# Turning the gated product with DVE blocks and DMAs through DRAM instead of TensorE transposes, in four feed-forwards

## The chip, the cores and the metric

The kernel runs on one core of one Trainium2 chip. The metric is the device time of one execution in microseconds (us), the median over several runs. PE is TensorE (its weight loads are shown apart as PEld), DVE is VectorE, ACT is ScalarE, POOL is GpSimd, and SP issues most of the DMAs.

## The reference

A two-layer trunk over 256 tokens of width 1024. Each layer is half a feed-forward, a token mixer, half a feed-forward; layer 0 mixes with a convolution module, layer 1 with latent attention. So there are four feed-forwards, all of this kind:

```
def swiglu_ffn(h, w1, w3, w2):
    return (jax.nn.silu(h @ w1) * (h @ w3)) @ w2
...
h = h + 0.5 * swiglu_ffn(rmsnorm(h, ffn_norm1[i]), ffn1_w1[i], ffn1_w3[i], ffn1_w2[i])
```

`w1` and `w3` are 1024 x 2816, `w2` is 2816 x 1024, everything in float32. The product `silu(..) * (..)`, 256 x 2816, is called the gated product here. The second multiplication contracts over its 2816 columns, so TensorE needs it with the columns on the partitions: it has to be turned.

## The kernel before

Float32 precision is reached with three matmuls for each product (`mm3`, L226 to L232): each operand is kept as a rounded part (`hi`, `Xh`, `Gh`) and a remainder (`lo`, `Xl`, `Gl`).

Weights come in blocks of 1 MB. SP loads each into a `raw` tile (three buffers), ACT rounds it into `hi` (L164), DVE makes `lo` (L165); `hi` and `lo` have four buffers each. SP issues its DMAs in the order in which they stand, and each waits there for its buffer, so a DMA at the head of SP's queue holds all behind it.

A feed-forward (`ffn_in`, L487) has two stages. The first goes over six chunks `c` of the 2816 columns: chunks 0 to 4 have 512 columns of `w1` and of `w3`, four weight blocks each; chunk 5 has 256 of each in two blocks. One block feeds 24 matmuls: 4 row tiles of the weights, two halves of 128 tokens (`tb`), three matmuls each. The four sums `u[m, tb]` of a chunk lie in the four PSUM banks of tag "A". After the chunk, ACT makes `s = silu(u[0, tb])` (L533) and DVE makes `g = s * u[1, tb]` (L535), 128 tokens x 512 columns, and a chunk's bank is free for a later one once its `s` and `g` are made. In chunk 5 both factors lie in one bank, so it uses two banks.

In `flush` PE transposes `g` in squares of 128 (L262, by `transposed`) into a PSUM bank of tag "B", four for a `g` of 512 columns and two for one of 256; ACT rounds the result into `Gh` (L497) and DVE writes `Gl` (L498). That is done early in the next chunk, for chunk 5 in the first block of the second stage.

The second stage (`Rows`) goes over 11 blocks of `w2`; block `i` contracts over column tiles 2i and 2i+1 of `Gh` and `Gl`. Its four sums `o` use the four "A" banks, the first two from chunk 4's later pair and the last two from chunk 5's. Blocks 9 and 10 are done in `finish`. Chunk 4's columns are needed from block 8 on, chunk 5's in block 10.

The order on each engine is set by a scheduler when the program is built, from the order of the code, from priorities (`urgent`) and from its own estimate of durations. Each engine then runs its instructions in that order.

Of the kernel before, what the change touches and what calls it, by code (L numbers as in the profile page):

```python
# [11 lines left out]
F32 = mybir.dt.float32  # L12
# [7 lines left out]
P = 128  # L20
# [59 lines left out]
def trunk(ctx: ExitStack, tc: tile.TileContext, x, pos, invf, gains, gfin, wdw,  # L80
          f1w13, f1w2, f2w13, f2w2, cw1, cw2, wa, wuq, wukv, wo, out):
    nc = tc.nc
# [4 lines left out]
    xp = ctx.enter_context(tc.tile_pool(name="x", bufs=1))  # L87
    tmp = ctx.enter_context(tc.tile_pool(name="tmp", bufs=2))
    small = ctx.enter_context(tc.tile_pool(name="small", bufs=4))
    ps = ctx.enter_context(tc.tile_pool(name="ps", bufs=1, space=bass.MemoryType.PSUM))  # L90

    n_uid = [0]

    def uid(s):
        n_uid[0] += 1
        return f"{s}_{n_uid[0]}"
# [4 lines left out]
    def bank(tag, name):  # L101
        return ps.tile([P, 512], F32, tag=tag, name=uid(name), bufs=BANKS[tag])
# [5 lines left out]
    for i in range(2):  # L108
        for w13, w2 in ((f1w13, f1w2), (f2w13, f2w2)):
# [6 lines left out]
            if w13 is f1w13:  # L116
                if i == 0:


                    for m in (-1, -2, 0, 1, 2, 3, 4, 5, 6, 7, -3, -4):  # L120
                        w = cw2[-m - 1] if m < 0 else cw1[m]
# [11 lines left out]
    def order(ins, first):  # L133
        tc.add_manual_dep(ins.ins, first.name, mybir.DependencyInfo(
            mybir.DependencyClass.NoSync, mybir.DependencyReason.DATA), reason="order")
# [45 lines left out]
    def load_ahead(ahead=W_BUFS - 2):  # L181
        load_to(min(len(blocks), n_used[0] + ahead))
# [5 lines left out]
    def weights(n=1, more=True):  # L188
        out = []
        for _ in range(n):  # L190
            n_used[0] += 1
            if more:
                load_ahead()
            else:
                load_ahead(0)
            out.append(loaded[n_used[0] - 1])
        return out
# [28 lines left out]
    def mm3(o, ah, al, bh, bl, start, stop, after=()):  # L226

        mm = nc.tensor.matmul(o, ah, bl, start=start, stop=False)  # L228
        for a in after:
            order(mm, a.ins)  # L230
        nc.tensor.matmul(o, ah, bh, start=False, stop=False)  # L231
        return nc.tensor.matmul(o, al, bh, start=False, stop=stop)  # L232

    def tbs(tb):
        return slice(tb * P, (tb + 1) * P)
# [23 lines left out]
    def transposed(src, q, n, after=(), turned=None):  # L259
        b = bank("B", "tp")  # L260
        for j in range(n):
            tp = nc.tensor.transpose(b[:, j * P:(j + 1) * P], src[:, (q + j) * P:(q + j + 1) * P], ident)  # L262
            if turned is not None:
                turned.append(tp)
            for a in after:
                order(tp, a.ins)
        return b
# [68 lines left out]
    class Plain:  # L336
# [22 lines left out]
        @urgent  # L359
        def turn(self, tb, q, after=()):  # L360
            b = bank("B", "tp")
            for j in range(4):
                mm = nc.tensor.matmul(b[:, j * P:(j + 1) * P], h[tb][:, (4 * q + j) * P:(4 * q + j + 1) * P],
                                      self.dg[tb], start=True, stop=True)
                for a in after:
                    order(mm, a.ins)
                self.turned.append(mm)
            for j in range(4):
                k = 4 * q + j
                g = G[:, self.col + k:self.col + k + 1]  # L370
                if j % 2 == 0:
                    nc.scalar.activation(self.x[:, k, tbs(tb)], b[:, j * P:(j + 1) * P], AF.Copy, scale=g)
                else:
                    nc.vector.tensor_scalar(self.x[:, k, tbs(tb)], b[:, j * P:(j + 1) * P], g, None, op0=ALU.mult)
# [108 lines left out]
    def ffn(X, make_next, beside=lambda: None):  # L483
        with tc.tile_pool(name=uid("ffn"), bufs=1) as act:
            return ffn_in(act, X, make_next, beside)

    def ffn_in(act, X, make_next, beside):  # L487
        Gh = act.tile([P, NF, S], F32R, tag="Gh", name=uid("Gh"))
        Gl = act.tile([P, NF, S], F32R, tag="Gl", name=uid("Gl"))
        pend = []  # L490

        def flush():
            for c, tb, w, g in pend:
                b = transposed(g, 0, w // P)
                f = slice(4 * c, 4 * c + w // P)
                bv = b[:, :w].rearrange("p (j t) -> p j t", t=P)
                nc.scalar.copy(Gh[:, f, tbs(tb)], bv)  # L497
                nc.vector.tensor_sub(Gl[:, f, tbs(tb)], bv, Gh[:, f, tbs(tb)].bitcast(F32))  # L498
            pend.clear()

        for c in range(6):

            both = c == 5
            w = 256 if both else 512
            kn = HB // 512
            u = {}
            for m in range(1 if both else 2):
                parts = weights(KT // kn, X.whole or c > 0 or m > 0)
                for tb in range(NT):
                    u[m, tb] = bank("A", "u")  # L510
                steps = [(k, tb) for k in range(KT) for tb in range(NT)]
                if not (X.whole and c == 0 and m == 0):
                    steps.sort(key=lambda t: (t[0] // kn, t[1]))
                if not X.whole and c == 0 and m == 0:
                    steps.sort(key=lambda t: t[1])
                for i, (k, tb) in enumerate(steps):
                    hi, lo = parts[k // kn]
                    j = k % kn
                    after = X.between if X.between and c == 0 and m == 0 and i == 2 else ()
                    mm = mm3(u[m, tb], X.xh[:, k, tbs(tb)], X.xl[:, k, tbs(tb)], hi[:, j * 512:(j + 1) * 512],  # L520
                             lo[:, j * 512:(j + 1) * 512], k == 0, k == KT - 1, after)
                    if X.whole and c == 0 and m == 0:
                        X.first(i, mm)
                    if c == 0 and m == 0 and i == (KT - 1 if X.between is None else 1):
                        X.late()
                        load_ahead()
                    if m == 0 and i == kn - 1:
                        flush()
                if c > 0:
                    beside()  # L530
            for tb in range(NT):
                s = tmp.tile([P, 512], F32, tag="s", name=uid("s"))
                nc.scalar.activation(s[:, :w], u[0, tb][:, :w], AF.Silu, scale=X.r[tb])  # L533
                g = tmp.tile([P, 512], F32, tag="g", name=uid("g"))
                nc.vector.tensor_mul(g[:, :w], s[:, :w], u[0, tb][:, w:] if both else u[1, tb])  # L535
                pend.append((c, tb, w, g))
        o = Rows(Gh, Gl, NF, make_next is Final)
        for i in range(NF // 2 - 2):
            o.block(i)
            if i == 0:  # L540
                flush()
            beside()
        return o.finish(X.rh, make_next, act)

# [492 lines left out]
    def beside():  # L1037

        for _ in range(4):
            next(todo, None)  # L1040
# [90 lines left out]
def build(shapes):  # L1131
    import concourse.bacc as _bacc

    nc = _bacc.Bacc("TRN2", target_bir_lowering=False, num_devices=1)
    args = [nc.dram_tensor(f"in_{n}", s, mybir.dt.from_np(np.dtype(d)), kind="ExternalInput").ap()
            for n, s, d in shapes]
    out = nc.dram_tensor("out", (S, D), F32, kind="ExternalOutput").ap()
    with tile.TileContext(nc, schedule_with_timeline_sim=True) as tc:
        trunk(tc, *args, out)
    return nc  # L1140
# [9 lines left out]
```

## Time and profile before

| | |
|---|---|
| median of 3 runs | 959.81 us (959.73 to 960.09) |
| the profiled execution | 959.79 us, span 958.0 us |
| PE busy | 947.2 us, 99% of the span |
| DVE, ACT, POOL busy | 551.2, 496.0, 86.1 us |
| granted TensorE clock | 0.999 |
| DMA | 167.41 MB, mean 175 GB/s |

The span is the time from the first to the last instruction of the program; the 1.8 us beside it lie around it. Busy times are unions of the instructions of one engine. A matmul's duration in the trace overlaps with the next one's, so what PE needs for one is read from the distance between starts, not from the duration.

### The profile page before, as it was taken

What the parts mean: (1) busy time and instruction counts of PE and PEld (TensorE: products, weight loads), DVE (VectorE), ACT (ScalarE), POOL (GpSimd) and SP (SyncE); (2) the same over time, 40 slices, a digit from 0 to 9 for tenths busy, and PEclk for the clock granted to TensorE, in tenths of its full rate; (3) what the DMA queues carried; (4) which work ended last, traced back from release to release, by engine and by line L of the source; (5) the groups of instructions that cost most, each with busy time, mean ns of one, the idle gap of its engine ahead of it and who ended that gap; (6) DMA issues with size and microseconds to landing.
All of it is one profiled execution on the core that took longest, in us unless ns stands there. A gap on an engine that the chain in (4) does not pass through costs nothing.

```text
span 958.0 us, 12026 instructions
## 1 busy us (share of the span) xinstructions
PE 947.2 (99%) x4588; PEld 790.3 (82%) x4588; DVE 551.2 (58%) x871; ACT 496.0 (52%) x852; POOL 86.1 (9%) x209
## 2 busy tenths in 40 slices
PE   9999999999999999999999999999999999999997
PEld 7888888898967888888888888888898788888885
DVE  6755554489975555554465555544766575555543
ACT  8844444368866444443364444434666574444431
POOL 1000000049920000000000000000200000000000
PEclk9999999999999999999999999999999999999999
DMA  8755446523315655555536555454441555555521
GB/s 315 278 197 184 176 176 210 187 89 133 132 45 222 218 179 186 199 183 181 204 141 222 176 181 198 176 193 143 173 179 45 198 220 176 180 192 199 176 88 45
DMA packets 25545, 167.41 MB, mean 175 GB/s; under 512 B 3216, under 2 KB 3600, under 8 KB 5904
## 3 DMA queue, kind: packets, MB, share of 16 engines
q1 hardware_dynamic: 24912, 165.83, 48.7%
q10 hardware_dynamic: 576, 0.82, 0.2%
q8 instruction: 36, 0.59, 0.2%
q14 instruction: 21, 0.17, 0.0%
HBM read 165.59 MB, written 1.05 MB: 174 GB/s over the span
## 4 chain that ended last, share of the span: by engine, by line
PE 93%; DVE 2%; ACT 2%; issue 1%; POOL 1%; DMA 0%; POOLq 0%; ACTq 0%; DVEq 0%
PE u L228 17%; PE u L232 17%; PE u L231 17%; PE o L228 10%; PE o L231 9%; PE o L232 9%; PE tp L262 3%; PE gate L566 3%; PE u L566 3%; PE o L750 1%; DVE lo L165 1%; DMA h<-in_x 0%; PE sc L968 0%; PE a L232 0%; PE a L228 0%
## 5 line engine op out<-in xcount | busy, mean ns | idle before, releaser
L165 DVE TENSOR_TENSOR lo<-raw,hi 128x1024 fp32r<-128x1024 f32 (+2 forms) x297 | 344.8, 1203 | 238.1 <-ACT hi L164 238.0
L164 ACT CAST hi<-raw 128x1024 fp32r<-128x1024 f32 (+2 forms) x297 | 292.7, 1038 | 268.4 <-PE u L232 115.7
L231 PE MATMUL u<-hi,Xh 128*128 128x512 f32 x704 | 276.3, 392 | 0.0
L232 PE MATMUL u<-hi,Xl 128*128 128x512 f32 x704 | 275.4, 392 | 0.4 <-DVE Xl L280 0.4
L228 PE MATMUL u<-lo,Xh 128*128 128x512 f32 x704 | 275.2, 391 | 0.0
L228 PEld LDWEIGHTS u<-lo,Xh 128*128 128x128 f32 x704 | 132.2, 188 | 27.5 <-DVE lo L165 0.4
L232 PEld LDWEIGHTS u<-hi,Xl 128*128 128x128 f32 x704 | 132.3, 188 | 27.2 <-DVE Xl L280 0.9
L231 PEld LDWEIGHTS u<-hi,Xh 128*128 128x128 f32 x704 | 132.2, 188 | 26.6
L231 PE MATMUL o<-hi,Gh 128*128 128x512 f32 (+1 forms) x356 | 138.6, 389 | 0.0
L232 PE MATMUL o<-hi,Gl 128*128 128x512 f32 (+1 forms) x356 | 137.8, 387 | 0.0
L228 PE MATMUL o<-lo,Gh 128*128 128x512 f32 (+1 forms) x356 | 136.7, 388 | 0.0
L228 PEld LDWEIGHTS o<-lo,Gh 128*128 128x128 f32 x356 | 66.9, 188 | 13.6
L232 PEld LDWEIGHTS o<-hi,Gl 128*128 128x128 f32 x356 | 66.9, 188 | 13.2
L231 PEld LDWEIGHTS o<-hi,Gh 128*128 128x128 f32 x356 | 66.9, 188 | 13.2
L253 POOL TENSOR_TENSOR ms<-ss 128x1 f32<-128x1 f32 x16 | 5.1, 318 | 658.2 <-ACT junk L248 658.2
L497 ACT CAST Gh<-tp 128x512 fp32r<-128x512 f32 (+1 forms) x48 | 26.3, 551 | 58.3 <-PE tp L262 58.3
L610 DVE SCALAR_TENSOR_TENSOR acc<-V,dw,acc 128x256 f32<-128x256 f32 (+1 forms) x160 | 54.0, 420 | 0.0
L498 DVE TENSOR_TENSOR Gl<-tp,Gh 128x512 fp32r<-128x512 f32 (+1 forms) x48 | 31.0, 647 | 36.6 <-ACT Gh L497 36.6
L535 DVE TENSOR_TENSOR g<-s,u 128x512 f32<-128x512 f32 (+1 forms) x48 | 30.7, 640 | 34.4 <-PE u L232 25.4
L628 ACT ACTIVATE prod<-V,dw 128x128 f32<-128x128 f32 (+1 forms) x121 | 46.3, 420 | 3.2 <-POOL odd L629 1.3
L533 ACT ACTIVATE s<-u,R 128x512 f32<-128x512 f32 (+1 forms) x48 | 31.2, 651 | 24.7 <-ACT hi L164 12.7
L280 DVE SCALAR_TENSOR_TENSOR Xl<-tp,G,Xh 128x128 fp32r<-128x128 f32 x80 | 22.1, 344 | 20.9 <-ACT Xh L276 20.9
(198 smaller groups left out, 836.2 us busy)
## 6 DMA issues: line engine op xcount, KB each, us to landing
raw<-in_f2w SPq DMA_DIRECT2D x66, 1024.0 KB, 4.8
raw<-in_f1w SPq DMA_DIRECT2D x64, 1024.0 KB, 4.8
raw<-in_cw SPq DMA_DIRECT2D x12, 1024.0 KB, 4.8
raw<-in_wo SPq DMA_DIRECT2D x4, 1024.0 KB, 5.0
raw<-in_wuq SPq DMA_DIRECT2D x3, 1024.0 KB, 5.0
raw<-in_f1w SPq DMA_DIRECT2D x8, 256.0 KB, 5.6
raw<-in_wa SPq DMA_DIRECT2D x2, 1024.0 KB, 4.7
raw<-in_wukv SPq DMA_DIRECT2D x2, 1024.0 KB, 5.6
```

The source lines that it names most:

```text
L164: behind(nc.scalar.copy(hi[:, c], raw[:, c]))
L165: behind(nc.vector.tensor_sub(lo[:, c], raw[:, c], hi[:, c].bitcast(F32)))
L228: mm = nc.tensor.matmul(o, ah, bl, start=start, stop=False)
L231: nc.tensor.matmul(o, ah, bh, start=False, stop=False)
L232: return nc.tensor.matmul(o, al, bh, start=False, stop=stop)
L262: tp = nc.tensor.transpose(b[:, j * P:(j + 1) * P], src[:, (q + j) * P:(q + j + 1) * P], ident)
L498: nc.vector.tensor_sub(Gl[:, f, tbs(tb)], bv, Gh[:, f, tbs(tb)].bitcast(F32))
L533: nc.scalar.activation(s[:, :w], u[0, tb][:, :w], AF.Silu, scale=X.r[tb])
L535: nc.vector.tensor_mul(g[:, :w], s[:, :w], u[0, tb][:, w:] if both else u[1, tb])
L566: mm = nc.tensor.matmul(u[:, t], w[:, c], X.x[:, k, t], start=(k == 0), stop=(k == KT - 1))
L610: nc.vector.scalar_tensor_tensor(out if j == j1 - 1 else y, v, w, y, op0=ALU.mult, op1=ALU.add)
L628: nc.scalar.activation(p, v, AF.Copy, scale=w)
```

## The change

`flush` and the list `pend` go. Each `g` is turned right after it is made:

- DVE turns it inside squares of 32 x 32 (one STREAM_TRANSPOSE) into `gt`; its input is read in such an order that the squares that belong to one partition group lie together.
- Four DMAs on SP's queue, one for each group of 32 partitions, write `gt` into a DRAM tile `gd`. The runs are 512 bytes long (256 for chunk 5), and the DRAM side is addressed so that the squares come to their places.
- One DMA on SP's queue reads `gd` back into `gb`, 128 partitions with 2 KB each (1 KB for chunk 5), once the four have landed.
- ACT makes `Gh` and DVE `Gl` as before, from `gb` in SBUF instead of from PSUM.

```diff
+    dram = ctx.enter_context(tc.tile_pool(name="dram", bufs=1, space=bass.MemoryType.DRAM))
...
-        pend = []
-
-        def flush():
-            for c, tb, w, g in pend:
-                b = transposed(g, 0, w // P)
-                f = slice(4 * c, 4 * c + w // P)
-                bv = b[:, :w].rearrange("p (j t) -> p j t", t=P)
-                nc.scalar.copy(Gh[:, f, tbs(tb)], bv)
-                nc.vector.tensor_sub(Gl[:, f, tbs(tb)], bv, Gh[:, f, tbs(tb)].bitcast(F32))
-            pend.clear()
+        def turn(c, tb, w, g):
+            n = w // P
+            t = act.tile([P, 512], F32, tag="gt", name=uid("gt"), bufs=2)
+            nc.vector.transpose(t[:, :w], g[:, :w].rearrange("p (t j q) -> p j t q", t=n, q=32))
+            d = dram.tile([P, w], F32, tag="gd", name=uid("gd"), bufs=4)
+            dv = d.rearrange("(j p) (i c) -> i p j c", p=32, c=32 * n)
+            for i in range(4):
+                nc.sync.dma_start(dv[i], t[32 * i:32 * i + 32, :w].rearrange("p (j c) -> p j c", j=4))
+            b = act.tile([P, 512], F32, tag="gb", name=uid("gb"), bufs=3)
+            nc.sync.dma_start(b[:, :w], d)
+            f = slice(4 * c, 4 * c + n)
+            bv = b[:, :w].rearrange("p (i t q) -> p t i q", i=4, q=32)
+            gh = Gh[:, f, tbs(tb)].rearrange("p t (i q) -> p t i q", q=32)
+            nc.scalar.copy(gh, bv)
+            nc.vector.tensor_sub(Gl[:, f, tbs(tb)].rearrange("p t (i q) -> p t i q", q=32), bv, gh.bitcast(F32))
...
-                    if m == 0 and i == kn - 1:
-                        flush()
...
-                pend.append((c, tb, w, g))
+                turn(c, tb, w, g)
...
-            if i == 0:
-                flush()
```

How the scheduler places it is shown at the end of chunk 4 and in chunk 5 of the first feed-forward; the other three look alike there. Lines from L500 to L507 are those of the new `turn`, and other lines move by one to four. The number behind a name is a running one.

On PE the transposes stood among chunk 5's matmuls, here the second group of four:

```order
L228 MATMUL u_1042<-lo_951,Xh_112 128x512
L262 MATMUL tp_1062<-ident,g_1023 128x128 x4
L231 MATMUL u_1042<-hi_950,Xh_112 128x512
L232 MATMUL u_1042<-hi_950,Xl_113 128x512
L228 MATMUL u_1042<-lo_951,Xh_112 128x512
```

Now nothing stands between the matmuls of the same chunk:

```order
L229 MATMUL u_1098<-lo_985,Xh_114 128x512
L232 MATMUL u_1098<-hi_984,Xh_114 128x512
L233 MATMUL u_1098<-hi_984,Xl_115 128x512
L229 MATMUL u_1098<-lo_985,Xh_114 128x512
L232 MATMUL u_1098<-hi_984,Xh_114 128x512
```

On SP's queue there were weight loads alone at this place:

```order
L155 DMA raw_1025<-in_f1w 128x2048
L155 DMA raw_1033<-in_f1w 128x2048
L155 DMA raw_1117<-in_f1w 128x2048
L155 DMA raw_1159<-in_f1w 128x2048
L155 DMA raw_1191<-in_f1w 128x2048
```

Now the eight writes and two reads of chunk 4's two turns stand between the loads `raw_1213`, `raw_1245` and `raw_1277`:

```order
L156 DMA raw_1213<-in_f1w 128x2048
L500 DMA gd_1057<-gt_1055 32x4x128 x4
L500 DMA gd_1072<-gt_1070 32x4x128 x4
L502 DMA gb_1062<-gd_1057 128x512
L156 DMA raw_1245<-in_f1w 128x2048
L502 DMA gb_1077<-gd_1072 128x512
L156 DMA raw_1277<-in_f1w 128x2048
```

On ACT the two `Gh` of chunk 4 stood ahead of a weight block's rounding and chunk 5's two `s`:

```order
L497 CAST Gh_184<-tp_1055 128x4x128
L497 CAST Gh_184<-tp_1062 128x4x128
L164 CAST hi_1118<-raw_1117 128x1024 x2
L533 ACTIVATE s_1105<-u_1041,R_286 128x256
L533 ACTIVATE s_1109<-u_1042,R_298 128x256
```

Now they stand later, each right ahead of one of chunk 5's `s`, and wait for a DMA instead of for PE:

```order
L165 CAST hi_1182<-raw_1181 128x1024 x2
L506 CAST Gh_186<-gb_1062 128x4x128
L539 ACTIVATE s_1147<-u_1097,R_288 128x256
L506 CAST Gh_186<-gb_1077 128x4x128
L539 ACTIVATE s_1162<-u_1098,R_300 128x256
```

## The prediction

> **What bounds the kernel now.** I read the page's busy times, slices and chain first, then PE's groups by shape and its timeline around one pair of transposes, then the room on the engines and queues that take the work over.
>
> ```profile
> PE 947.2 (99%) x4588; PEld 790.3 (82%) x4588; DVE 551.2 (58%) x871; ACT 496.0 (52%) x852; POOL 86.1 (9%) x209
> PE   9999999999999999999999999999999999999997
> PEclk9999999999999999999999999999999999999999
> PE 93%; DVE 2%; ACT 2%; issue 1%; POOL 1%; DMA 0%; POOLq 0%; ACTq 0%; DVEq 0%
> PE u L228 17%; PE u L232 17%; PE u L231 17%; PE o L228 10%; PE o L231 9%; PE o L232 9%; PE tp L262 3%; PE gate L566 3%; PE u L566 3%; PE o L750 1%; DVE lo L165 1%; DMA h<-in_x 0%; PE sc L968 0%; PE a L232 0%; PE a L228 0%
> ```
>
> PE has no slice with a hole, the chain that ends last is PE for 93%, and the clock is full throughout. So PE's own instructions, one after the other, are the time, and whatever leaves PE in the feed-forwards shortens the kernel, as long as nothing new makes PE wait. The transposes (`tp L262`) are on that chain.
>
> **What the removal gives.** The first row is a group by shape, the others PE's timeline in chunk 4's end and chunk 5 of the second feed-forward (start, duration), then DVE's timeline with the first `g` of chunks 3 and 4.
>
> ```profile
> L262 PE MATMUL tp<-ident,g 128*128 128x128 f32 x176 | 26.8, 272 | 0.0
> ...
> 407.71 0.39 PE L232 MATMUL u<-hi,Xl 128*128 128x512 f32 x1
> ...
> 413.60 0.39 PE L231 MATMUL u<-hi,Xh 128*128 128x512 f32 x1
> 413.83 0.60 PE L262 MATMUL tp<-ident,g 128*128 128x128 f32 x4
> 414.19 0.48 PE L232 MATMUL u<-hi,Xl 128*128 128x512 f32 x1
> 414.50 0.39 PE L228 MATMUL u<-lo,Xh 128*128 128x512 f32 x1
> ...
> 386.10 0.68 DVE L535 TENSOR_TENSOR g<-s,u 128x512 f32<-128x512 f32 x1
> 408.82 0.68 DVE L535 TENSOR_TENSOR g<-s,u 128x512 f32<-128x512 f32 x1
> ```
>
> All 176 transposes of `g` go: 40 groups of four and 8 of two. From 407.71 to 413.60 lie 26 steps of 0.2265 us, the price of one matmul. With four transposes, 413.60 to 414.50 takes 0.90 where two plain steps take 0.45: a group of four costs 0.45. The duration of 272 ns overlaps; the start distances say about 0.11 each. A group of two is 0.22 less, 0.23. The sum is 40 x 0.45 + 8 x 0.23 = 19.8 us. A second way: chunk 4's `g` comes 22.72 us after chunk 3's, and 96 matmuls at 0.2265 to 0.227 are 21.8; the 0.93 left over, 20 times, and half of it for the four chunks 5, are 20.5 us. I take 20.0.
>
> [...]
>
> **What is added on DVE and ACT.** DVE gets 48 block transposes, which the trace does not show. The nearest rows are DVE's passes over the same 128x512 float32:
>
> ```profile
> L535 DVE TENSOR_TENSOR g<-s,u 128x512 f32<-128x512 f32 x40 | 27.4, 685 | 25.4 <-PE u L232 25.4
> L498 DVE TENSOR_TENSOR Gl<-tp,Gh 128x512 fp32r<-128x512 f32 x40 | 27.6, 692 | 32.3 <-ACT Gh L497 32.3
> L497 ACT CAST Gh<-tp 128x512 fp32r<-128x512 f32 x40 | 23.4, 588 | 49.9 <-PE tp L262 49.9
> 388.00:410.00 22.00, 22.00 (x103) 18.20 (x102) 12.12 (x12) 10.46 (x12) 0.00 (x0) 1.00 0.51 187
> ```
>
> I take 0.7 us each, between half of it and, should the reordering cost a second pass, 1.4. Two per chunk are 1.4 us (0.7 to 2.8) beside DVE's 12.1 busy in a window of 22 us (the third busy figure; ACT's 10.5 follows): hidden, with the 10 us idle as cover. `Gh` and `Gl` stay two passes of the same size; reading SBUF instead of PSUM I cost at nothing, by `lo`'s rows below, where 1024 columns from SBUF take 1.18 us each. The fewer waits for PE on ACT are worth nothing, since ACT is not the bound.
>
> **What is added on SP and the DMA engines.** SP gets 240 DMAs, ten per chunk.
>
> ```profile
> SPq L155 <- DVE lo L165: 648.0, 123, 19.7
> 408.94 0.33 SPq L155 DMA_DIRECT2D raw<-in_f2w  x1
> raw<-in_f2w SPq DMA_DIRECT2D x66, 1024.0 KB, 4.8
> out<-hg SPq DMA_DIRECT2D x1, 256.0 KB, 2.1
> out<-hg SPq DMA_DIRECT2D x2, 128.0 KB, 2.2
> pi<-in_pos SPq DMA_DIRECT2D x1, 1.0 KB, 6.4
> 32.00:54.00 22.00, 22.00 (x102) 18.27 (x102) 15.30 (x17) 14.34 (x23) 0.00 (x0) 1.00 0.81 299
> ```
>
> SP sits idle for most of the span, 648 us of it waiting for DVE to free a `raw` buffer; ten issues of 0.33 are 3.3 us of a chunk. Bytes: a chunk moves 4 MB of weights, and now 0.5 MB out and 0.5 MB back, 5 MB in 21.8 us or 240 GB/s; in the window from 32 to 54 the engines moved 299 with PE at 22.00 of 22.00, so bandwidth is hidden too.
>
> What can bite is latency. A store to DRAM on a quiet queue landed in 2.1 to 2.2 us. The 1 KB of `pi`, issued behind weight loads at the start, took 6.4: on one queue a small DMA waits for the large ones ahead. So each of a turn's two steps lands in 2.2 to 6.4. Usually one of the two meets one load of 4.8, so I take 2.2 and 4.8.
>
> Two things are queued behind these waits. **On SP**, the next weight load waits until `gd` has landed. The cover is the lead of the weights: the load issued at 408.94 lands 4.8 later, at 413.7.
>
> ```profile
> 406.55 2.36 DVE L165 TENSOR_TENSOR lo<-raw,hi 128x1024 fp32r<-128x1024 f32 x2 [3.08 <-ACT hi L164]
> 410.86 0.69 DVE L535 TENSOR_TENSOR g<-s,u 128x512 f32<-128x512 f32 x1 [1.35 <-PE u L232]
> 410.86 2.01 ACT L164 CAST hi<-raw 128x1024 fp32r<-128x1024 f32 x2 [3.39 <-PE u L232]
> 417.23 2.00 ACT L164 CAST hi<-raw 128x1024 fp32r<-128x1024 f32 x2 [0.57 <-PE u L232]
> 420.03 0.47 ACT L533 ACTIVATE s<-u,R 128x256 f32<-128x256 f32 x1 [0.79 <-ACT hi L164]
> 422.75 0.47 ACT L533 ACTIVATE s<-u,R 128x256 f32<-128x256 f32 x1 [2.25 <-PE u L232]
> 423.12 1.99 ACT L164 CAST hi<-raw 128x1024 fp32r<-128x1024 f32 x2
> ```
>
> That load refills the buffer that `lo` freed at 408.91; with three buffers its rounding is the third from there (410.86, 417.23, 423.12), 9.4 us after it lands. The rounding itself runs when PE has released the fourth block back, so three blocks of 24 x 0.227 = 5.45 us still lie ahead of PE: 16.3, less about 4.4 for `hi` and `lo`. A load may come some 21 us late before PE notices.
>
> **On ACT and DVE**, `Gh` and `Gl` of one chunk now stand ahead of the next chunk's `s` and `g`, which free the PSUM banks. For chunks 0 to 4 the next `s` is due 20 us later. The tight place is chunk 5, two blocks or 10.9 us long. Chunk 4 ends at 410.7 (PE's last `u`, which released the `g` at 410.86); call that T. The second turn of chunk 4: `g` done T + 0.9, DVE turn T + 1.6, four issues T + 2.9, landed T + 5.1 (T + 9.3 if behind loads), issue and read T + 10.2 (T + 16.0), `Gh` T + 10.8 (T + 16.6). The second `s` of chunk 5 behind it cannot begin before T + 11.1 anyway. PE needs its bank for the fourth `o`, 18 matmuls into the second stage: T + 10.9 + 4.1 = T + 15.0, and `s` and `g` take 0.47 and 0.42. With my values it is in time by some 3 us; with both ends at 6.4 it is late by 2.5. I cost it at nothing, 0 to 2.5 per feed-forward. Chunk 5's own turns are not needed before block 10, some 50 us on.
>
> **The sum.** Removed 19.8 to 20.5; added on PE's path 0, at most 4 x 2.5 = 10. The profiled execution took 959.79 (span 958.0, 1.8 around it), 0.02 below the median. 959.8 - 20.0 = 939.8, and 0.2 for small shifts outside the feed-forwards: **940.0 us**.
>
> **Rivals.**
>
> *The turn is late at chunk 5* (chance 0.14). For it speaks `pi` at 6.4, against it that two waits behind full loads are needed in one turn. ACT and DVE then hold chunk 5's `s` and `g`, and PE waits for banks at the fourth `o`. Price 2.5 us in each feed-forward at the bound: 940 + 10 = 950, still faster.
>
> *SP becomes the bound, and the kernel slower* (0.05). In each chunk SP waits for two landings, issues ten DMAs (3.3 us) and four loads (1.3 us). That fits in 21.8 us up to a landing of (21.8 - 4.6) / 2 = 8.6 us each. Beyond it the weights fall behind in every chunk and PE ends up waiting for `hi`. At 10 us each a chunk takes 24.6, 2.8 more than PE needs, 56 us over the 20 chunks: 996 us. From 9.1 us on (1 us per chunk) the gain is eaten. Against it: no landing in the rows above, queued or not, reaches 8.6.
>
> [...]
>
> *The time doesn't move* (0.03): PE's freed time turns into another wait of just that size, such as on ACT's `hi` (a chunk's four are 8 us of ACT). Against it speaks the window from 388 to 410 with ACT and DVE idle half the time. Time 958 to 961.
>
> **Chances and range.** 0.78 for the forecast, which I let reach from 938.5 (the 20.5 and a little) to 943. Within 943 to 958 lies the first rival; its bound is 950 and half of it below 948. The range 938.5 to 948 leaves out about 0.16. Faster by over 0.2% (about what a measurement of this kernel can tell from no change, 1.9 us): 0.78 + 0.14 = 0.92; same 0.03; slower 0.05.
>
> **What would show it.** In the profile after: no `tp<-ident,g` on PE, `g` of consecutive chunks 21.8 us apart instead of 22.72, PE still at 99%. STREAM_TRANSPOSE at about 0.7 us. The writes `gd` landing in 2 to 5 us, `gb` in 2 to 6. ACT's `Gh` waiting for `gb` for some us in places, and PE without a wait at the first `o`. It is wrong if the chunk period stays above 22.2, if PE shows waits for `hi`, `lo` or `g`, or if SP's loads come later than 21 us after their buffer is free.

## The result, and the profile after

The changed kernel takes 938.49 us in the median (938.24 to 941.18, four runs) against 959.92 us (959.73 to 960.09) for the kernel before on the same chip: a ratio of 0.9781, 95% interval 0.9769 to 0.9793. That is 21.4 us less, where 20 were forecast. The profiled execution took 938.43 us, span 936.6 us.

The page of the kernel after, its busy times, PE's slices, the chain and the DMA queue:

```profile
PE 926.3 (99%) x4412; PEld 773.4 (83%) x4412; DVE 578.9 (62%) x919; ACT 494.8 (53%) x852; POOL 85.9 (9%) x209
PE   9999999999999999999999999999999999999997
PE 93%; DVE 2%; ACT 2%; issue 1%; POOL 1%; DMA 0%; POOLq 0%; ACTq 0%; DVEq 0%
DMA packets 60106, 190.49 MB, mean 203 GB/s; under 512 B 11152, under 2 KB 33040, under 8 KB 40464
q1 hardware_dynamic: 59472, 188.91, 58.4%
```

PE has 176 instructions less and is busy for 20.9 us less; it still has no slice with a hole and is still 93% of the chain. DVE is busy for 27.7 us more. The engine that bounded the kernel bounds it still, with less to do.

The new work by shape (busy time and mean ns of one, then the idle time ahead of it), the issues of its DMAs (the last column is the median from issue to landing in us), and ACT's and DVE's waits for it (total us, times, longest):

```profile
L496 DVE STREAM_TRANSPOSE gt<-g 128x512 f32<-128x512 f32 x40 | 28.4, 711 | 1.2
L496 DVE STREAM_TRANSPOSE gt<-g 128x256 f32<-128x256 f32 x8 | 3.6, 446 | 0.3
L507 DVE TENSOR_TENSOR Gl<-gb,Gh 128x512 fp32r<-128x512 f32 x40 | 27.5, 689 | 30.7 <-ACT Gh L506 30.7
```

```profile
raw<-in_f2w SPq DMA_DIRECT2D x66, 1024.0 KB, 5.0
gd<-gt SPq DMA_DIRECT2D x160, 64.0 KB, 3.1
gb<-gd SPq DMA_DIRECT2D x40, 256.0 KB, 5.0
```

```profile
ACT Gh L506 <- DMA gb<-gd: 59.4, 31, 5.8
DVE Gl L507 <- ACT Gh L506: 45.8, 29, 4.7
```

The block transpose costs DVE 711 ns, about as much as its pass for `Gl` over the same size, 689. The four writes of a turn land in 3.1 us, the read in 5.0. ACT stands idle for 59.4 us until a `gb` lands. PE waits for none of it; these are all of its waits (same columns):

```profile
PE warm L221 <- DVE still L216: 1.0, 1, 1.0
PE tp L263 <- DMA h<-in_x: 0.8, 1, 0.8
PE o L754 <- ACT Z L690: 0.8, 1, 0.8
PE u L233 <- DVE Xl L281: 0.4, 1, 0.4
PE rb L683 <- DVE dg L681: 0.2, 1, 0.2
```

Where the time came from shows in the length of each stage, read from PE's timeline as the distance from the first `u` matmul to the first `o` matmul, and from there to the next part of the program (for the last, to its last `o`):

| us | before | after | difference |
|---|---|---|---|
| first stages, feed-forwards 1 to 4 | 125.71, 125.42, 125.09, 125.80 | 121.25, 120.62, 120.30, 120.99 | 4.46, 4.80, 4.79, 4.81 |
| second stages, 1 to 4 | 62.18, 61.63, 61.63, 60.39 | 61.66, 61.11, 61.11, 59.87 | 0.52 each |

These eight differences add up to 20.9 of the 21.4 us. A first stage held ten groups of four transposes, 0.48 us each (the first one's 4.46 holds the program's start); a second stage two groups of two, 0.26 each. The convolution and the attention between them took the same to 0.05 us.

### The profile page after: what moved, and what is told of

The parts are those of the page before. It is cut to its first block, busy times and chain, and to the rows that moved or that the text cites. A ratio compares the mean times of both kernels' runs of the same rounds, so it can differ in the third digit from the quotient of the medians.

```text
span 936.6 us, 12106 instructions
## 1 busy us (share of the span) xinstructions
PE 926.3 (99%) x4412; PEld 773.4 (83%) x4412; DVE 578.9 (62%) x919; ACT 494.8 (53%) x852; POOL 85.9 (9%) x209
## 4 chain that ended last, share of the span: by engine, by line
PE 93%; DVE 2%; ACT 2%; issue 1%; POOL 1%; DMA 0%; POOLq 0%; ACTq 0%; DVEq 0%
PE u L229 17%; PE u L233 17%; PE u L232 17%; PE o L229 10%; PE o L232 10%; PE o L233 10%; PE gate L570 3%; PE u L570 3%; PE o L754 2%; PE tp L263 1%; DVE lo L166 1%; DMA h<-in_x 0%; PE sc L972 0%; PE a L233 0%; PE a L229 0%
## 5 line engine op out<-in xcount | busy, mean ns | idle before, releaser
L506 ACT CAST Gh<-gb 128x512 fp32r<-128x512 f32 (+1 forms) x48 | 28.0, 584 | 59.4 <-DMA gb<-gd 59.4
L507 DVE TENSOR_TENSOR Gl<-gb,Gh 128x512 fp32r<-128x512 f32 (+1 forms) x48 | 30.9, 645 | 45.9 <-ACT Gh L506 45.8
```

The costliest lines, as they stand in the source:

```text
L506: nc.scalar.copy(gh, bv)
L507: nc.vector.tensor_sub(Gl[:, f, tbs(tb)].rearrange("p t (i q) -> p t i q", q=32), bv, gh.bitcast(F32))
```

## The experiments

In the expectations, A is the explanation behind the forecast: PE lost just the slots of its transposes, and the transport through DVE, SP, DRAM and ACT is hidden. Theory B, or the rival, is the other explanation of the run at hand. Ratios are to the kernel before, on the same chip.

| run | median us | range | ratio, 95% interval |
|---|---|---|---|
| kernel after, again | 938.39 | 938.06 to 938.64 | 0.9768, 0.9754 to 0.9783 |
| transposes back, idle | 959.54 | 959.26 to 961.69 | 0.9994, 0.9985 to 1.0003 |
| no turn at all | 938.58 | 938.40 to 940.45 | 0.9775, 0.9760 to 0.9789 |
| one more trip through DRAM | 940.94 | 940.15 to 941.88 | 0.9798, 0.9782 to 0.9815 |
| three more trips | 974.62 | 970.00 to 976.56 | 1.0143, 1.0114 to 1.0171 |
| turn's DMAs on POOL | 938.90 | 938.69 to 940.87 | 0.9782, 0.9768 to 0.9797 |
| turn's DMAs on ACT | 940.27 | 939.01 to 940.50 | 0.9788, 0.9772 to 0.9804 |
| chunk 4 late | 938.64 | 937.95 to 939.85 | 0.9776, 0.9762 to 0.9791 |
| chunk 4 late, PE's order pinned | 956.74 | 953.58 to 959.30 | 0.9962, 0.9948 to 0.9975 |

The kernel after once more, beside the first five:

> The changed kernel itself, as the mark for the other runs on this chip: 938.5 us (938.2 to 938.8 undisturbed).

It took 938.39 us, span 936.8.

### The transposes put back, with nobody reading them

```diff
+        pend = []
+
+        def idle():
+            for w, g in pend:
+                transposed(g, 0, w // P)
+            pend.clear()
...
+                    if m == 0 and i == kn - 1:
+                        idle()
...
                 turn(c, tb, w, g)
+                pend.append((w, g))
...
+            if i == 0:
+                idle()
```

> The changed kernel, with the 176 transposes of g put back on PE at their old places, and nobody reading their result. Theory A (PE's slots are the whole gain, the transport is free): the time returns to that of before, 958 to 960. The prediction's price of a group (0.45 for four, 0.23 for two, 19.8 in all) would give 958.3; the price by chunk period, with slow steps behind the group, 959.9. Theory B (a part of the gain came from the PSUM reads of Gh and Gl that also went, the steps of 0.23 to 0.24 behind each group): those slow steps, some 0.034 per group or 1.6 us in all, stay away, so 958.3, and the steps behind a group are 0.2265 again.

959.54 us: 21.15 of the 21.7 us by which the kernel before is longer on this chip (960.07) come back, and the interval of the ratio holds 1, though ACT and DVE no longer read the transposes' banks. PE's timeline of this run at a group in the second feed-forward (start, duration):

```profile
413.45 0.39 PE L232 MATMUL u<-hi,Xh 128*128 128x512 f32 x1
413.68 0.60 PE L263 MATMUL tp<-ident,g 128*128 128x128 f32 x4
414.03 0.48 PE L233 MATMUL u<-hi,Xl 128*128 128x512 f32 x1
414.35 0.39 PE L229 MATMUL u<-lo,Xh 128*128 128x512 f32 x1
414.58 0.40 PE L232 MATMUL u<-hi,Xh 128*128 128x512 f32 x1
414.81 0.40 PE L233 MATMUL u<-hi,Xl 128*128 128x512 f32 x1
415.05 0.40 PE L229 MATMUL u<-lo,Xh 128*128 128x512 f32 x1
```

From 413.45 to 414.35 two matmuls and the four transposes take 0.90 us, as in the kernel before. The matmul right behind the group takes 0.32 to the next, and the three after it 0.23, 0.23 and 0.24. Over all groups of this run these four steps are 0.315, 0.230, 0.234 and 0.233 us in the mean (in the kernel before, over 38 groups of four, 0.315, 0.230, 0.234 and 0.235), where a plain one is 0.2265. A plain rival for the slow steps was that ACT and DVE read PSUM just then; here they read SBUF and the steps stay. They belong to the transposes.

### No turn at all

`Gh` and `Gl` are made from the unturned `g`: no block transpose, no DMA, and the columns that the second stage contracts are the wrong ones, in the same shapes.

```diff
-            t = act.tile([P, 512], F32, tag="gt", name=uid("gt"), bufs=2)
...
-            nc.sync.dma_start(b[:, :w], d)
...
-            bv = b[:, :w].rearrange("p (i t q) -> p t i q", i=4, q=32)
+            bv = g[:, :w].rearrange("p (i t q) -> p t i q", i=4, q=32)
```

> The changed kernel without any turn: Gh and Gl are made from g as it stands, with no block transpose and no DMA, so the feed-forwards multiply an unturned product. It is the floor that a free transport would reach. Theory A: 938.5, within 0.5 of the changed kernel. Rival (the transport costs PE something, by late banks or by late weights): 1 to 5 us lower.

938.58 us, span 936.6, the same as the kernel after. From the second feed-forward to the third the stages are 120.62, 61.11, 120.30 and 61.11 us, equal to those after in every digit. So the whole transport, 48 passes of DVE, 240 DMAs and 23 MB, costs nothing in the feed-forwards, and this is the floor for any way to turn `g` off PE that leaves PE's other work as it is.

### How much cover is left: one and three more trips

Each turn's tile is copied once, or three times, from DRAM to DRAM before it is read back.

```diff
+            d2 = dram.tile([P, w], F32, tag="gd2", name=uid("gd2"), bufs=4)
+            nc.sync.dma_start(d2, d)
...
-            nc.sync.dma_start(b[:, :w], d)
+            nc.sync.dma_start(b[:, :w], d2)
```

```diff
+            for k in range(3):
+                d2 = dram.tile([P, w], F32, tag="gd2", name=uid("gd2"), bufs=12)
+                nc.sync.dma_start(d2, d)
+                d = d2
```

> Each turn makes one more trip, DRAM to DRAM, between the write and the read back: one more landing of 3 to 5 us, waited for on SP. The scheduler now puts only the first Gh of chunk 4 ahead of a due s of chunk 5. Theory A (SP has slack up to a landing of some 8 us, and chunk 5 keeps its slack by that order): 938.5, no change; SP's wait for DVE's lo falls by some 100 us. Rival (the turn's latency is already near its limit): 2 to 3 us per feed-forward, 947 to 950.

> Each turn makes three more trips through DRAM, so that SP waits for four landings in a row and issues 16 DMAs in a chunk. Theory A with the prediction's rule for SP: four landings of 4 to 5 us, 16 issues and four loads of 0.33 each make 22.6 to 26.6 us of a chunk of 21.8, so SP becomes the bound: 1 to 5 us per chunk, 960 to 1040, with PE waiting for hi or lo. Rival (SP's waits never reach PE, since the turns of two chunks overlap in its queue and loads slip between): 938.5.

With one more trip the stages of the second and third feed-forward are again 120.62, 61.11, 120.30 and 61.11. The 2 us more lie in the program's first 10 us, ahead of any turn: the first `u` matmul starts at 8.32 instead of 6.92, at double steps (8.89, 9.32, 9.74). From 10.06 on they are 0.23 to 0.24, and the kernel after has none above 0.33 at this place. Steps of 0.43 us stand beside a granted clock of 0.50 in the run with three more trips (429 to 430 us), but here the profile has 1.00 in the windows from 8 to 10 us, so what makes them was not shown. Single runs of the kernels before and after show an excess of that size too (962.64, 941.18). But all four runs of this kernel have it (940.15 to 941.88), so whether the edit brings it stays open; what is shown is that the stages with the turns lose nothing.

With three more trips the kernel is 1.4% slower than before. SP's, PE's and ACT's waits of that run (total us, times, longest):

```profile
SPq L156 <- DVE lo L166: 224.5, 68, 19.8
SPq L504 <- DMA gd<-gd: 183.1, 75, 5.8
```

```profile
PE o L229 <- DVE g L545: 23.0, 6, 8.0
```

```profile
ACT Gh L510 <- DMA gb<-gd: 269.7, 47, 10.4
```

SP does wait for the landings, 183.1 us at that line alone, but it still sits 224.5 us waiting for `raw` buffers to come free, and PE never waits for `hi` or `lo`: the weights aren't late for PE. The first stages are 120.96, 121.75, 120.30 and 121.89 us, within 1.2 of those after. What gives way are the second stages: 66.72, 69.58, 66.88 and, to the end of the program, 77.32, where the kernel after has 61.66, 61.11, 61.11 and 66.87. PE waits for `g`. The long waits, 3.2, 6.1, 4.0 and 8.0 us, one in each feed-forward, are ahead of the third sum, which takes the first bank that chunk 5 frees; the two others are under 1 us.

### The queue that carries the turn

```diff
-                nc.sync.dma_start(dv[i], t[32 * i:32 * i + 32, :w].rearrange("p (j c) -> p j c", j=4))
+                nc.gpsimd.dma_start(dv[i], t[32 * i:32 * i + 32, :w].rearrange("p (j c) -> p j c", j=4))
...
-            nc.sync.dma_start(b[:, :w], d)
+            nc.gpsimd.dma_start(b[:, :w], d)
```

The second run has `nc.scalar` in both places.

> The turn's ten DMAs per chunk are issued by POOL instead of SP. Theory A (nothing of the transport is on PE's path): 938.5, no change, and SP waits for lo as long as before (some 640 us). If small DMAs wait behind weight loads because they share SP's queue, gd and gb land sooner on another one, near the 2.1 to 2.2 us of the quiet stores; if they share the engines' bandwidth alone, they stay at 3.1 and 5.0.

> The turn's DMAs are issued by ACT. ACT's queue then holds its casts and silus while it waits for a landing: two waits of 3 us and ten issues of 0.35 per chunk, some 10 us beside 10.5 of work in 21.8. Theory A (the cover is the lead of the weights and the slack of the banks): it just fits, 938.5 to 942. Rival (a wait in front of computing work is paid in full at the banks): 2 to 6 us per chunk, 980 or more.

The DMA issues with POOL's queue, and with ACT's:

```profile
gd<-gt POOLq DMA_DIRECT2D x160, 64.0 KB, 3.0
gb<-gd POOLq DMA_DIRECT2D x40, 256.0 KB, 4.8
```

```profile
gd<-gt ACTq DMA_DIRECT2D x160, 64.0 KB, 3.1
gb<-gd ACTq DMA_DIRECT2D x40, 256.0 KB, 2.8
```

The writes land as on SP's queue, 3.0 to 3.1 us, so it isn't the weight loads ahead of them in SP's queue that make them longer than the 2.2 us of a lone store. The read is the same from POOL and shorter from ACT, so for it the question stays open: ACT issues at other times (its first read at 38.0 us, SP's at 36.1), and an issue of the read takes 0.57 us on POOL where SP's takes 0.34, which may hide a gain. Neither run is faster. On ACT's queue ACT stands still behind the landings, and PE does not notice:

```profile
ACT hi L165 <- DMA gd<-gt: 141.1, 17, 9.9
```

Its second feed-forward's first stage is 120.62 us, as after; what the run has more lies in the start again (first `u` matmul at 8.95, its step 0.45, the next 0.24).

### The deadline at chunk 5

The turns of chunk 4 alone make one more trip, and chunk 5's `s` is kept behind chunk 4's `Gh` on ACT:

```diff
+            if c == 4:
+                d2 = dram.tile([P, w], F32, tag="gd2", name=uid("gd2"), bufs=4)
+                nc.sync.dma_start(d2, d)
+                d = d2
...
+                sa = nc.scalar.activation(s[:, :w], u[0, tb][:, :w], AF.Silu, scale=X.r[tb])
+                if c == 5:
+                    order(sa, hold[4, tb][0].ins)
```

> One more trip for chunk 4's two turns alone, and the order on ACT pinned so that each s of chunk 5 stands behind the matching Gh of chunk 4. It tests the tight place of the prediction. Theory A: the second read lands at T + 14 to T + 16 (T is the end of chunk 4), Gh, s and g follow by T + 15.5 to T + 17.5 against a deadline of T + 15.0, so PE waits 0.5 to 2.5 us at the second stage's fourth sum in each feed-forward: 940.5 to 948.5, and the wait is seen on PE at o. Rival (the banks are free earlier than worked out, or PE has other slack): 938.5.

938.64 us and no wait on PE: a miss for A. The second `g` of chunk 5 was late, even more than meant. DVE's timeline in the second feed-forward:

```profile
420.54 0.69 DVE L513 TENSOR_TENSOR Gl<-gb,Gh 128x512 fp32r<-128x512 f32 x1 [2.44 <-ACT Gh L512]
421.15 0.41 DVE L549 TENSOR_TENSOR g<-s,u 128x256 f32<-128x256 f32 x1
```

It ends at 421.56, which is 19.5 us after chunk 4's end (T), 4.5 past the deadline of the forecast. But the scheduler, which sees the longer way when it sets the order, had moved PE's matmuls. This is the order of the first `o` matmuls in all four feed-forwards of each kernel (a to d are the four sums, in the order in which they start; the number is how many matmuls of a sum stand in a row):

```
before                   a6 b6 a1 c6 a3 d
after                    a6 b6 a4 c6 a2 d
chunk 4 late             a6 b6 a6 b6 a1 c12 a5 d
chunk 4 late, pinned     a6 b6 c6 d
```

The fourth sum, d, needs the bank that the second `g` of chunk 5 frees. With 42 matmuls ahead of it instead of 24 it starts at 412.93 + 42 x 0.2265 = 422.44, 0.9 us after the `g`. So the last run keeps the late chunk and pins PE's order: no matmul of the second block before all four sums have had the first.

```diff
+                    mm = self.mm(part, i, tb, d, self.o[tb, d], 0, self.nk - (4 if apart else 0),
+                                 after=self.done if i == 1 else ())
+                    if i == 0:
+                        self.done.append(mm)
```

> The kernel of the run before (one more trip for chunk 4's turns, each s of chunk 5 behind chunk 4's Gh), with PE's order pinned too: no matmul of the second stage's block 1 before all four sums have had block 0. Theory A (the deadline of the prediction, T + 15.0, is right for that order, and the run before escaped it because the scheduler had put 13 matmuls of blocks 1 and 2 ahead of the third sum): there the second g of chunk 5 ended at T + 19.5, so PE waits some 4.5 us at the fourth sum in each feed-forward, 18 us in all, and up to 1.5 us more each if the granted clock falls as it did after the waits with three more trips: 956 to 963. Rival (PE has other slack at the banks, and the order had nothing to do with it): 938.5.

956.74 us, 18 more than with the free order. PE's waits, and PE and DVE in the second feed-forward:

```profile
PE o L229 <- DVE g L554: 11.8, 4, 3.9
```

```profile
419.09 0.39 PE L233 MATMUL o<-hi,Gl 128*128 128x512 f32 x1
423.43 0.50 PE L229 MATMUL o<-lo,Gh 128*128 128x512 f32 x1 [3.95 <-DVE g L554]
...
424.57 0.63 PE L232 MATMUL o<-hi,Gh 128*128 128x512 f32 x1
424.99 0.63 PE L233 MATMUL o<-hi,Gl 128*128 128x512 f32 x1
...
427.87 0.40 PE L229 MATMUL o<-lo,Gh 128*128 128x512 f32 x1
428.10 0.40 PE L232 MATMUL o<-hi,Gh 128*128 128x512 f32 x1
```

```profile
422.35 0.69 DVE L518 TENSOR_TENSOR Gl<-gb,Gh 128x512 fp32r<-128x512 f32 x1 [2.18 <-ACT Gh L517]
422.96 0.41 DVE L554 TENSOR_TENSOR g<-s,u 128x256 f32<-128x256 f32 x1
```

The first `o` of this stage starts at 415.24; 18 matmuls later, at 419.32, the fourth sum is due, and PE stops there until `g` ends at 423.37. It happens once in each feed-forward. The second stages are 2.8, 5.9, 2.8 and 4.7 us longer than with the free order, 16.2 together: 11.8 of waiting, and 4.4 beyond the waits, most of it slow matmuls behind the two longer ones. So the place and the time fit theory A, but its split does not: it had 4.5 us of waiting in each feed-forward, and the waits are 2.5 to 3.95. The profiled execution, 954.53 us, is among the shorter of the ten.

## Why the prediction was right, and where it was off

**The gain is PE's slots alone: shown.** Putting the transposes back returns 21.15 of 21.7 us, and taking the transport away gains nothing (938.58 against 938.39).

**The price of a group was too small.** The sum had 0.45 us for four and 0.23 for two, 19.8 in all. The stages give 0.48 and 0.26: 19.2 + 2.1 = 21.3. Reading a single group cost almost nothing: the stretch from the matmul ahead of it to the second one behind it takes 0.90 us there, and 0.903 in the mean over the 38 groups of four that stand alone in the kernel before (0.899 to 0.909). Most of the 0.03 us missing for a group of four lies behind the place where the reading stopped: the next three matmuls are slow as well, 0.02 us together. (Priced by a transpose's duration, 272 ns, the 176 would have been 48 us; putting them back cost 21.15.) The second way, from the period of `g`, saw the whole: 22.72 less 96 x 0.2265 is 0.98 per chunk. It was taken with 0.227 for the upper bound of a step, which ate part of it. The period after is 21.76, two `g` of one half in consecutive chunks:

```profile
378.13 0.68 DVE L541 TENSOR_TENSOR g<-s,u 128x512 f32<-128x512 f32 x1
399.89 0.68 DVE L541 TENSOR_TENSOR g<-s,u 128x512 f32<-128x512 f32 x1
```

This term, with the 0.2 us for shifts elsewhere that didn't come, is the 1.5 us by which 940.0 lies above 938.5. The measured 938.49 us lies on the lowest edge of the forecast's range, 938.5 to 948: the mechanism held, but that the size stayed in the range was luck.

**The landings.** 2.2 and 4.8 us were taken, 3.1 and 5.0 measured. The row used for the small writes was a store with nothing beside it. Both are within the bounds given, and hidden. The reading of `pi`'s 6.4 us, that a small DMA waits for the large ones ahead on its queue, is not what lengthens the writes: on POOL's queue they take 3.0.

**The turn's timetable at chunk 5 held, its deadline didn't.** The kernel after in the second feed-forward, ACT first, then DVE and PE:

```profile
412.45 0.62 ACT L506 CAST Gh<-gb 128x512 fp32r<-128x512 f32 x1 [1.85 <-DMA gb<-gd]
412.98 0.47 ACT L539 ACTIVATE s<-u,R 128x256 f32<-128x256 f32 x1
```

```profile
401.92 0.69 DVE L541 TENSOR_TENSOR g<-s,u 128x512 f32<-128x512 f32 x1 [0.60 <-PE u L233]
402.64 0.71 DVE L496 STREAM_TRANSPOSE gt<-g 128x512 f32<-128x512 f32 x1
...
413.71 0.41 DVE L541 TENSOR_TENSOR g<-s,u 128x256 f32<-128x256 f32 x1
```

```profile
412.60 0.39 PE L229 MATMUL o<-lo,Gh 128*128 128x512 f32 x1
```

T is 412.60 less 10.87 for chunk 5's 48 matmuls, 401.7. The read ends at 412.4, T + 10.7 where T + 10.2 was forecast, and the `g` behind it at T + 12.4. But "18 matmuls into the second stage" was counted as if each sum took its first block's six in turn. The order of the kernel after has 24, the deadline is T + 16.3, and the margin is 3.9 us instead of the forecast 3. For the order with 18 the forecast deadline is shown: pinned to it, PE stops at T + 15.0.

**The rule for SP was wrong in kind.** The second rival added two landings per chunk in a row and let SP fail from 8.6 us each. With five landings in each turn it still doesn't fail. SP waits for the landings 256 us in all (`gd<-gd` 183.1 and 71.1, `gd<-gt` 1.5), 10.7 in each of the 24 chunks, where four landings of 4 to 5 us in a row would be 16 to 20: in SP's queue the DMAs of two turns stand between each other, so while SP waits for one turn's tile, the other's is already on its way. SP has 224.5 us left. The first rival's place, chunk 5's banks, is the one that gives way first, and the 10 us that the prediction gave as its price are a bound only for two landings of up to 6.4 us. With three more trips the same place makes the kernel slower than before, 974.62 us, which the prediction allowed only to SP.

## What to carry to other kernels

Price a small PE instruction among large ones by the distance between starts up to where the steps are plain again, not up to the next matmul, and over whole stages: here that is 0.48 us against the 0.45 of one group. Here the transport cost nothing with its last step 3.9 us ahead of the instruction that needs the bank (0.9 us with chunk 4 late), and 18 us in all with that step 2.5 to 4 us behind in each feed-forward, so look for the stage with the least time between the two (here the short last chunk) and read the real order there before counting. A scheduler that knows of the delay can move that deadline itself, as it did here, and an experiment on such a margin has to pin the order.

## What the runs showed of the hardware that was not expected

Two of PE's four waits in the pinned run cost 1.9 us more than their length. The steps behind the 3.95 us wait are 0.43 us instead of 0.23 for some eight matmuls. The granted clock behind the waits of the first, second and fourth feed-forward (the last three figures of a row are clock, DMA share and GB/s):

```profile
135.00:138.00 3.00, 3.00 (x14) 2.46 (x14) 0.61 (x2) 1.51 (x2) 0.00 (x0) 1.00 0.96 351
424.00:427.00 3.00, 3.00 (x9) 2.38 (x8) 0.22 (x1) 1.30 (x2) 0.00 (x0) 0.55 0.50 151
889.00:892.00 3.00, 3.00 (x9) 2.34 (x8) 0.00 (x0) 1.01 (x2) 0.00 (x0) 0.51 0.66 211
```

The waits ahead of them, as PE's timeline has them (the first of these and the one in the third feed-forward, 2.52, are alike):

```profile
134.75 0.50 PE L229 MATMUL o<-lo,Gh 128*128 128x512 f32 x1 [2.48 <-DVE g L554]
888.22 0.56 PE L229 MATMUL o<-lo,Gh 128*128 128x512 f32 x1 [2.85 <-DVE g L554]
```

After 2.48 and 2.52 us the clock stays full (1.00 in the 3 us behind each) and the stage grows by 0.3 us beyond the wait; after 2.85 and 3.95 it is halved for some 3 us (0.51 and 0.55 in the windows above) and the stage grows by 1.9 beyond. A bound on the length between 2.52 and 2.85 us fits these four waits, as an estimate from them alone: no run shows that the length is what decides. The ten runs of this kernel, of which one has a trace, took from 953.58 to 954.82 us with a mean granted clock of 0.995 and from 956.26 to 959.30 with 0.992 to 0.994; behind which waits the clock fell in the others was not shown.

The turn's bytes were dearer for the DMA engines than the weights: on POOL's queue its 23.08 MB, in runs of 0.25 to 2 KB, took 7.9% of their time, 2.9 MB per percent, where the weight loads' queue in the same run has 165.83 MB in 49.3%, 3.4 per percent. Whether the length of the runs makes the difference no run shows. The weight loads beside the turn went from 4.8 to 5.0 us in the kernel after, and PE did not wait for that.
